# Matmul with RMS norm: transposes copied by two engines, two matmuls of a product placed earlier, and a reordered end

## The chip, the cores and the metric

The kernel runs on one core of a Trainium2 chip. The metric is the device time of one execution in microseconds (us), from the measured runs; the profile is of one further execution, taken by the hardware profiler. Engines are named as the profile names them: PE is TensorE (PEld its weight loads), DVE is VectorE, ACT is ScalarE, POOL is GpSimd and SP is SyncE. A bank is one of the eight parts of PSUM, the memory that PE writes; a tile of 128 x 512 fp32 fills one.

## The reference

```python
def setup_inputs():
    m, k, n = 2048, 2048, 2048
    return {
        "a": np.random.randn(m, k).astype(np.float32),
        "b": np.random.randn(k, n).astype(np.float32),
        "gamma": np.random.randn(n).astype(np.float32),
        "eps": np.float32(1e-5),
    }

def reference(a, b, gamma, eps):
    x = np.matmul(a, b)
    rms = np.sqrt(np.mean(x ** 2, axis=-1, keepdims=True) + eps)
    return (gamma * x / rms).astype(np.float32)
```

## The kernel before, in words

The 2048 rows of A are 16 row blocks of 128. The contraction is cut into 16 tiles of 128, taken in pairs: `kp` runs over 8 pairs. The 2048 columns are four chunks of 512, two to a half. PE needs A transposed, with the contraction on the partitions, so each 128x128 piece of A is turned by PE itself (a matmul with `is_transpose`) into PSUM and copied to SBUF, or is turned by a DMA later on. B arrives as bf16, in `raw[half][kp]`.

The order of the work is written out by hand (`manual_schedule`): each engine executes its instructions in the order of the program text. The program writes no semaphores; the tile layer derives the waits from the tiles that instructions read and write. `tbank` and `acc[0]` to `acc[6]` are the eight banks.

**Head, left half of the columns.** Row blocks 0 to 3 are multiplied while A and B are still loading. For each `kp`, `stream` issues 14 matmuls of 128x512 (seven pairs of row block and chunk, two tiles of the contraction) into `acc`. After the first `when` of them it calls `transpose_head(kp + 1)`: eight transposes (L182) into `tbank`, viewed as bf16 `(t, r, m)` with the two tiles `t` side by side in one bank, and one DVE copy (L187) of 128x1024 into `head_at`. The eighth pair of row block and chunk has no bank of its own: `stream_in_parts` computes it by two matmuls (L435) in `tbank`, the same bank as the transposes, and DVE adds it to an SBUF tile (L442; ACT copies it the first time, L439). After that DVE forms differences of quarters of B for later (`b_diff`, `b_rest`). The loads of A (`early`, L119) and B (L115) are issued by POOL, one behind the other. `transpose_first` (L167) does the first pair from fp32, with one bank for DVE and one for ACT. After the last `kp`, ACT and DVE evict the seven banks by turns (L445).

**Head, right half.** `stream_right(kp)` computes rows blocks 0 and 1 plainly (`first` and `second`, four matmuls each, into `acc[0]` to `acc[3]`) and, for row blocks 2 and 3, products of a Strassen-Winograd scheme: seven products of sums of quarters in place of eight. `product_matmul(g, j, m, bank, kp, start)` issues step `kp` of product `m` (L358); `product` runs all eight. Product 1 gathers in bank `u2`, product 2 in `u4`, product 7 in `p7`. Afterwards (L517 to L546) ACT copies `u2` to `x11`, product 6 is added into `u2`, DVE copies that to `u4`, products 3 and 5 follow. ACT evicts the first plain bank and then computes two row norms of the next row blocks (`row_norm`, L220); DVE turns these into scales (`row_factor`, L230) and scales A to fp16 (`row_apply`, L241), and PE transposes it (`transpose_half`, L195).

**Middle.** Pairs of row blocks go through the seven products, with sums, squares, norms and stores of earlier rows beside them (`segment`); some groups add a second level of the scheme (`step`, L397). The change does not touch this part.

**End.** `last_group` (L752) orders the last products, `do(n, m)`, by hand. `B2` and `B3` are banks; `b3[1]` holds the upper right result after product 5 of the right half, until ACT copies it to `x22[1]` (L810); product 3 of that half then accumulates into the same bank. `square_of` squares a chunk on ACT and sums it along the row. The last row block needs its whole sum of squares, then a root on ACT (L288) and a reciprocal on DVE (L293); the factor `r_b` scales four chunks: one on DVE (L855, with a store of its own), chunks 1 and 3 of the tile `wide` on ACT (`by_r`, L766, two instructions) and chunk 2 on DVE (L762). One store of 768 KB (L860) takes the last three.

Of the kernel before, what the change touches and what calls it, by code (L numbers as in the profile page):

```python
# [17 lines left out]
def kernel(  # L18
# [13 lines left out]
    nc = tc.nc  # L32
# [4 lines left out]
    KP = KT // 2  # L37
    W2 = 2 * P
    MB = M // P
    CH = 512  # L40
# [137 lines left out]
    def transpose_head(kp):  # L178
        view = tbank.bitcast(BF16).rearrange("p (t r m) -> p t r m", t=2, r=HB)
        for t in range(2):  # L180
            for r in range(HB):
                nc.tensor.matmul(  # L182
                    view[:, t, r, :], ah(kp)[:, r, t * P:(t + 1) * P], identity,
                    is_transpose=True,
                    start=(t == 0 and r == 0), stop=(t == 1 and r == HB - 1),
                )
        nc.vector.tensor_copy(out=head_at[:, 2 * kp:2 * kp + 2, :, :], in_=view)  # L187

    a16 = {}

# [74 lines left out]
    def x_chunk(mb, c):  # L265
        return x_tile(mb, c // 2)[:, (c % 2) * CH:(c % 2 + 1) * CH]
# [181 lines left out]
    for kp in range(KP):  # L448
        if kp + 4 < KP:
            load_head(kp + 4)  # L450
        else:
            load_later(1)
        before = [lambda: transpose_head(kp + 1)] if kp + 1 < KP else []
        if kp == KP - 2:
            before.append(lambda: a_sums(PAIR, (3,), False))
        stream(kp, before, len(groups1) + {0: 5, 1: 3}.get(kp, 2))
        if kp == KP - 1:
            evict(groups1, "ADADADA")
        stream_in_parts(last1, kp)
        if kp > 0:  # L460
            b_diff(0, kp - 1)
        if 0 < kp < KP - 2:
            b_rest(0, kp - 1)
# [8 lines left out]
    def stream_right(kp):  # L472
        first, second = ([(g, 2 * kp + t) for g in plain] for t in range(2))
        if kp == 0:
            for both in zip(first, second):
                for g, kt in both:
                    head_matmul(banks[g], *g, kt)
            product_matmul(PAIR, 1, 1, u2, kp, True)
            product_matmul(PAIR, 1, 2, u4, kp, True)
            return  # L480
        product_matmul(PAIR, 1, 1, u2, kp, True)
        for g, kt in first:
            head_matmul(banks[g], *g, kt)
        if kp == KP - 1:
            product_matmul(PAIR, 1, 7, p7, kp - 1, True)
        product_matmul(PAIR, 1, 2, u4, kp, True)
        if kp < KP - 1:
            product_matmul(PAIR, 1, 7, p7, kp - 1, True)
        for g, kt in second:
            head_matmul(banks[g], *g, kt)  # L490

    for kp in range(KP):
        load_later(1)
        b_diff(1, kp)
        stream_right(kp)
        if kp % 2 == 0:
            square_half(kp // 2, 0)
        if kp > 0:
            b_rest(1, kp - 1)
        if kp == 0:  # L500
            b_diff(0, KP - 1)
            b_rest(0, KP - 3)
        if kp == 1:
            b_rest(0, KP - 2)
            b_rest(0, KP - 1)
        if kp in (2, 3, 4):
            a_sums(PAIR, ((1,), (2,), (4,))[kp - 2])
# [4 lines left out]

    r2, r3 = HB - 2, HB - 1
    x11, x12, x21, x22 = (x_chunk(r, c) for r in (r2, r3) for c in (2, 3))
    copy_on("A")(out=x11, in_=u2)  # L517
    product_matmul(PAIR, 1, 7, p7, KP - 1, True)
    b_rest(1, KP - 1)
    add(x11, u4, x11)  # L520
    evict(plain[:1], "A")
    row_norm(HB)
    row_norm(HB + 1)
    product(PAIR, 1, 6, u2, start=False)
    nc.vector.tensor_copy(out=u4, in_=u2)
    row_factor(HB)
    row_apply(HB)
# [224 lines left out]
    def last_group():  # L752
        n = len(halves) - 2
        g = NG - 1
        ra, rb = 2 * g, 2 * g + 1
        x11, x12, x21, x22 = zip(chunks(n), chunks(n + 1))
        xa, xb = x_tile(ra, 0), x_tile(rb, 0)
        gam = [gamma_sb[:, c * CH:(c + 1) * CH] for c in range(NCH)]
        gam_left = gamma_sb[:, 0:HALF]

        def scaled_gamma(x, src, r, gamma_of_x):
            nc.vector.scalar_tensor_tensor(out=x, in0=src, scalar=r, in1=gamma_of_x,  # L762
                                           op0=ALU.mult, op1=ALU.mult)

        def by_r(x, r):
            nc.scalar.activation(out=x, in_=x, func=ACTF.Copy, scale=r)  # L766

        def by_r_pool(x, r):
            nc.gpsimd.tensor_scalar(out=x, in0=x, scalar1=r, scalar2=1.0,  # L769
                                    op0=ALU.mult, op1=ALU.mult)  # L770

        b2, b3 = [B2[(n + j) % 2] for j in range(2)], [B3[(n + j) % 2] for j in range(2)]
        x00, x01 = first_sums(n)[0:2]
        do(n, 6)
        step(g - 1, 1, X2)
        nc.scalar.copy(out=W2, in_=X2)
        square_right(rb - 2)
        do(n - 1, 3)
        step(g - 1, 2, W2)
        step(g - 1, 6, X2)  # L780
        nc.scalar.copy(out=Y2, in_=X2)
        finish(rb - 2)
        take(n - 1, 12)
        add(x00, W2, x00)
        do(n + 1, 1)
        step(g - 1, 5, Y2)
        step(g - 1, 7, W2)
        step(g - 1, 4, X2)
        square_half(ra - 2, 0)
        add(x11[1], Y2, x11[1])  # L790
        a_sums(g, (4,))
        add(x11[0], W2, x11[0])
        add(x11[1], W2, x11[1])
        take_pre(ra - 2)
        square_of(ra, x11[1])
        do(n, 5)
        nc.scalar.copy(out=x22[0], in_=b3[0])
        add(x11[0], X2, x11[0])
        step(g - 1, 3, Y2)
        add(x01, Y2, x01)  # L800
        square_right(ra - 2)
        do(n + 1, 6)
        finish(ra - 2)
        do(n, 7)
        add(x22[0], x21[0], x22[0])
        add(b2[0], b2[0], x21[0])
        square_of(rb, x22[0])
        add(x11[1], x11[1], gam[2], ALU.mult)
        do(n + 1, 5)
        nc.scalar.copy(out=x22[1], in_=b3[1])  # L810
        wide = a_pool.tile([P, K], FP32, name="a32")
        chunk = [wide[:, c * CH:(c + 1) * CH] for c in range(NCH)]
        add(chunk[1], x22[0], gam[1], ALU.mult)
        pre_b = stat_pool.tile([P, 1], FP32, name="part")
        add(pre_b, msq[rb][:, 0:1], msq[rb][:, 1:2])
        do(n, 3)
        take(n, 12)
        square_half(ra, 0)
        pre_a = stat_pool.tile([P, 1], FP32, name="pre")
        nc.vector.tensor_scalar(out=pre_a, in0=msq[ra][:, 0:1], scalar1=msq[ra][:, 1:2],  # L820
                                scalar2=msq[ra][:, 2:3], op0=ALU.add, op1=ALU.add)
        add(xa, xa, gam_left, ALU.mult)
        do(n + 1, 3)
        take(n + 1, 12)
        square_of(ra, x12[1])
        rms_a = root(msq[ra][:, 3:4], pre_a)
        r_a = inverse(rms_a)
        other = X2
        product(g, 1, 7, other)
        nc.scalar.copy(out=x21[1], in_=other)  # L830
        left, mid = xa[:, 0:CH], xa[:, CH:]
        by_r(left, r_a)
        nc.sync.dma_start(out=rows(ra, 0, CH), in_=left)
        by_r_pool(mid, r_a)
        nc.sync.dma_start(out=rows(ra, CH, HALF), in_=mid)
        by_r_pool(x11[1], r_a)
        add(b2[1], b2[1], x21[1])
        add(x22[1], x21[1], x22[1])
        scaled_gamma(x12[1], x12[1], r_a, gam[3])
        nc.sync.dma_start(out=rows(ra, HALF, N), in_=x_tile(ra, 1))  # L840
        do(n, 4)
        square_of(rb, b2[0])
        square_of(rb, x22[1])
        add(xb[:, 0:CH], b2[0], gam[0], ALU.mult)
        part = stat_pool.tile([P, 1], FP32, name="part")
        nc.vector.tensor_scalar(out=part, in0=pre_b, scalar1=msq[rb][:, 2:3],
                                scalar2=msq[rb][:, 3:4], op0=ALU.add, op1=ALU.add)
        add(chunk[3], x22[1], gam[3], ALU.mult)
        do(n + 1, 4)
        last_sq = stat_pool.tile([P, 1], FP32, name="last_sq")  # L850
        sq = sq_pool.tile([P, 2 * CH], BF16, name="sq")
        nc.scalar.activation(out=sq[:, 0:CH], in_=b2[1], func=ACTF.Square, scale=inv_sqrt_n,
                             accum_out=last_sq)
        r_b = inverse(root(last_sq, part))
        nc.vector.tensor_scalar_mul(out=xb[:, 0:CH], in0=xb[:, 0:CH], scalar1=r_b)  # L855
        nc.sync.dma_start(out=rows(rb, 0, CH), in_=xb[:, 0:CH])
        for c in (1, 3):
            by_r(chunk[c], r_b)
        scaled_gamma(chunk[2], b2[1], r_b, gam[2])
        nc.sync.dma_start(out=rows(rb, CH, N), in_=wide[:, CH:])  # L860

# [38 lines left out]
```

## Time and profile before

| | |
|---|---|
| median of 3 runs (lowest to highest) | 219.31 us (219.22 to 220.76) |
| profiled execution | 219.36 us |
| its span, first to last instruction | 217.6 us |
| PE busy | 207.6 us, 95% of the span |
| DVE busy | 161.6 us, 74% |
| ACT busy | 113.3 us, 52% |
| POOL busy | 35.3 us, 16% |
| granted PE clock, mean | 0.99 |

In the lines of the profile, `L187 DVE COPY head_at<-tbank 128x1024 bf16<-128x1024 bf16 x7` is line 187 of the kernel, the engine, the operation, the tile written and the tile read, their shapes, and how often. Lines of a timeline begin with the start and the duration in us and end, in brackets, with the idle time of the engine just before and what ended it; neighbouring instructions of one kind are merged into one line. Durations of matmuls overlap, since PE is pipelined: 512 columns show about 0.38 us each and start 0.216 us apart. PEld is the weight load ahead of a matmul. The chain that ended last is followed back from the last instruction, at each step to what released it.

### The profile page before, as it was taken

The numbers are of one execution on the slowest core, as the hardware profiler recorded it, in microseconds if no ns is written. First come the engines' busy times: TensorE is split into PE (matmuls) and PEld (weight loads), VectorE is DVE, ScalarE is ACT, GpSimd is POOL, SyncE is SP. The second block draws the span as 40 slices with busy tenths as digits, with TensorE's granted clock in tenths as the row PEclk, the third lists the DMA queues.
The fourth block names the chain that finished last, engine by engine and source line by source line (L and its number), as shares of the span: only waits on it lengthen the run. The fifth ranks groups of instructions, "written<-read, shape, count | busy, mean of one in ns | idle before, by whom it ended". The sixth has DMA issues, their size and how long they took to land.

```text
span 217.6 us, 2966 instructions
## 1 busy us (share of the span) xinstructions
PE 207.6 (95%) x1016; PEld 95.9 (44%) x1016; DVE 161.6 (74%) x323; ACT 113.3 (52%) x223; POOL 35.3 (16%) x74
## 2 busy tenths in 40 slices
PE   7899999999999999999999999999999999999970
PEld 3344544444455444444444444444444444444420
DVE  1227769999899997788975899399856985475771
ACT  2110001910599579498626962594728951555772
POOL 7644434434001000100021001100101000000020
PEclk9999999999999999999999999999999999999996
DMA  7999999999969798978674975497596992040454
GB/s 151 167 200 204 203 205 209 209 211 211 399 220 358 295 264 230 334 294 240 163 234 167 350 246 99 184 245 240 118 268 237 326 261 50 0 193 3 193 191 195
DMA packets 37039, 46.60 MB, mean 214 GB/s; under 512 B 22560, under 2 KB 26656, under 8 KB 35744
## 3 DMA queue, kind: packets, MB, share of 16 engines
q0 software_dynamic: 10608, 23.86, 45.5%
q1 hardware_dynamic: 26144, 22.29, 33.7%
q10 hardware_dynamic: 272, 0.26, 0.3%
q8 instruction: 8, 0.13, 0.2%
q14 instruction: 7, 0.06, 0.1%
HBM read 34.60 MB, written 16.78 MB: 236 GB/s over the span
## 4 chain that ended last, share of the span: by engine, by line
PE 85%; DMA 9%; POOL 2%; issue 1%; ACT 1%; ACTq 0%; DVE 0%; POOLq 0%
PE acc L358 65%; PE acc L406 11%; DMA early<-in_a_dram 5%; DMA b<-in_b_dram 4%; PE acc L397 3%; PE tbank L397 2%; POOL b L115 1%; PE tbank L358 1%; PE tbank L435 1%; PE tbank L182 1%; POOL early L119 1%; PE tbank L195 0%; PE acc L195 0%; ACT a L766 0%; ACTq L895 0%
## 5 line engine op out<-in xcount | busy, mean ns | idle before, releaser
L358 PEld LDWEIGHTS <-s 128*128 128x128 f16 (+1 forms) x312 | 30.5, 98 | 37.0 <-DVE s L335 0.3
L272 ACT ACTIVATE sq<-x 128x1024 bf16<-128x1024 f32 (+1 forms) x33 | 33.2, 1005 | 24.8 <-DVE x L101 20.9
L406 PE MATMUL acc<-b,head_at 128*128 128x512 bf16 x176 | 43.0, 379 | 0.9 <-DMA b<-in_b_dram 0.7
L311 DVE SCALAR_TENSOR_TENSOR x<-x,r,gamma_sb 128x1024 f32<-128x1024 f32 x28 | 34.9, 1282 | 0.5
L358 PE MATMUL acc<-b,head_at 128*128 128x512 bf16 x136 | 33.9, 379 | 0.0
L101 DVE TENSOR_TENSOR x<-acc,x 128x512 f32<-128x512 f32 x33 | 22.3, 687 | 11.4 <-PE acc L358 5.4
L358 PEld LDWEIGHTS <-head_at 128*128 128x128 f16 (+1 forms) x192 | 18.7, 98 | 22.2
L358 PE MATMUL acc<-b,at_even 128*128 128x512 bf16 x112 | 26.3, 379 | 0.0
L406 PEld LDWEIGHTS <-head_at 128*128 128x128 bf16 x176 | 16.9, 98 | 20.1 <-issue 1.0
L358 PE MATMUL acc<-early,s 128*128 128x512 bf16 x104 | 25.5, 379 | 0.0
L358 PE MATMUL acc<-b,s 128*128 128x512 bf16 x104 | 24.6, 379 | 0.0
L358 PEld LDWEIGHTS <-at_even 128*128 128x128 f16 x160 | 15.6, 98 | 18.6
L224 ACT ACTIVATE sq<-a 128x1024 bf16<-128x1024 f32 x22 | 23.3, 1058 | 0.6 <-DMA a<-in_a_dram 0.2
L358 PE MATMUL acc<-t_left,s 128*128 128x512 bf16 x96 | 22.7, 379 | 0.0
L115 POOL DMA_DIRECT2D b<-in_b_dram x32 | 17.2, 541 | 20.4 <-DMA b<-in_b_dram 14.3
L445 ACT COPY x<-acc 128x512 f32<-128x512 f32 x7 | 4.0, 581 | 25.8 <-PE acc L406 25.8
L587 ACT COPY acc<-acc 128x512 f32<-128x512 f32 x12 | 6.9, 576 | 10.4 <-PE acc L358 10.4
L187 DVE COPY head_at<-tbank 128x1024 bf16<-128x1024 bf16 x7 | 4.8, 691 | 8.1 <-PE tbank L182 8.1
L293 DVE RECIPROCAL r<-rms 128x1 f32<-128x1 f32 x16 | 2.6, 160 | 10.6 <-ACT rms L288 10.6
L101 DVE TENSOR_TENSOR x<-tbank,x 128x512 f32<-128x512 f32 x9 | 6.2, 690 | 4.2 <-PE tbank L435 4.1
L589 ACT COPY x<-acc 128x512 f32<-128x512 f32 x10 | 5.9, 585 | 5.3 <-PE acc L358 5.3
L769 POOL TENSOR_SCALAR x<-x,r 128x512 f32<-128x512 f32 x2 | 1.4, 691 | 41.9 <-DVE r L293 41.9
(129 smaller groups left out, 240.5 us busy)
## 6 DMA issues: line engine op xcount, KB each, us to landing
out_dram<-x SPq DMA_DIRECT2D x29, 512.0 KB, 3.0
a<-in_a_dram POOLq DMA_DIRECT2D x9, 1024.0 KB, 5.5
b<-in_b_dram POOLq DMA_DIRECT2D x32, 256.0 KB, 9.9
a<-in_a_dram POOLq DMA_DIRECT2D x4, 512.0 KB, 10.0
early<-in_a_dram POOLq DMA_DIRECT2D x7, 256.0 KB, 10.2
gamma_sb<-in_gamma_dram POOLq DMA_DIRECT2D x2, 512.0 KB, 10.1
head_at<-in_a_dram POOLq DMA_DIRECT2D x1, 1024.0 KB, 8.2
out_dram<-x SPq DMA_DIRECT2D x3, 256.0 KB, 2.6
```

What stands on the lines that cost most here:

```text
L101: nc.vector.tensor_tensor(out=out, in0=in0, in1=in1, op=op)
L115: nc.gpsimd.dma_start(out=raw[j][kp][:, t, :], in_=b[lo:lo + P, j * HALF:(j + 1) * HALF])
L187: nc.vector.tensor_copy(out=head_at[:, 2 * kp:2 * kp + 2, :, :], in_=view)
L224: nc.scalar.activation(out=junk, in_=a32[mb][:, h * HALF:(h + 1) * HALF], func=ACTF.Square, scale=2.0 ** -8, accum_out=n2[:, h:h + 1])
L272: nc.scalar.activation(out=sq[:, 0:src.shape[-1]], in_=src, func=ACTF.Square, scale=inv_sqrt_n, accum_out=msq[mb][:, c:c + 1])
L311: nc.vector.scalar_tensor_tensor(out=x, in0=x, scalar=inverse_of[mb], in1=gamma_sb[:, h * HALF:(h + 1) * HALF], op0=ALU.mult, op1=ALU.mult)
L358: nc.tensor.matmul(bank, lhsT[:, kp, :], rhs, start=(start and kp == 0), stop=(kp == KP - 1), skip_group_check=not start)
L397: nc.tensor.matmul(bank, lhsT[:, k, :], rhs, start=(m in (1, 7) and k == 0), stop=(k == KQ - 1), skip_group_check=m not in (1, 7))
L406: nc.tensor.matmul(bank, head_at[:, kt, r, :], head_rhs(c, kt), start=(kt == 0), stop=(kt == KT - 1))
L445: copy_on(engine)(out=x_chunk(*g), in_=banks[g])
L587: nc.scalar.copy(out=b3, in_=b2)
L589: nc.scalar.copy(out=chunks(n)[2], in_=B7)
```

## The change

It has five edits in three places.

In `transpose_head` the one DVE copy of both tiles becomes a DVE copy of tile 0 and an ACT copy of tile 1. In the loop over `kp`, the transposes stand behind 10 of the 14 matmuls for every `kp` from 1 (before: 10 for `kp` 1 and 9 from `kp` 2), and behind 12 for `kp` 0 as before.

In `stream_right`, at the last `kp`, the ACT copy of `u2` stands behind `first` in program order, and the first two matmuls of product 6 follow product 7, ahead of product 2 and `second`. The loop after it issues the other six.

In `last_group` the copy of `b3[1]` to `x22[1]` goes ahead of the square of `x22[0]` on ACT, and the two scalings of chunks 1 and 3 become one instruction over both.

```diff
@@ transpose_head @@
-        nc.vector.tensor_copy(out=head_at[:, 2 * kp:2 * kp + 2, :, :], in_=view)
+        nc.vector.tensor_copy(out=head_at[:, 2 * kp, :, :], in_=view[:, 0])
+        nc.scalar.copy(out=head_at[:, 2 * kp + 1, :, :], in_=view[:, 1])
@@ loop over kp @@
-        stream(kp, before, len(groups1) + {0: 5, 1: 3}.get(kp, 2))
+        stream(kp, before, len(groups1) + (5 if kp == 0 else 3))
@@ stream_right @@
         if kp == KP - 1:
+            copy_on("A")(out=x11, in_=u2)
             product_matmul(PAIR, 1, 7, p7, kp - 1, True)
+            for k in range(2):
+                product_matmul(PAIR, 1, 6, u2, k, False)
         product_matmul(PAIR, 1, 2, u4, kp, True)
@@ after the loop over stream_right @@
-    copy_on("A")(out=x11, in_=u2)
     product_matmul(PAIR, 1, 7, p7, KP - 1, True)
...
-    product(PAIR, 1, 6, u2, start=False)
+    for kp in range(2, KP):
+        product_matmul(PAIR, 1, 6, u2, kp, False)
@@ last_group @@
-        square_of(rb, x22[0])
         add(x11[1], x11[1], gam[2], ALU.mult)
         do(n + 1, 5)
         nc.scalar.copy(out=x22[1], in_=b3[1])
+        square_of(rb, x22[0])
...
-        for c in (1, 3):
-            by_r(chunk[c], r_b)
+        by_r(wide.rearrange("p (c n) -> p c n", n=CH)[:, 1::2, :], r_b)
```

The lines that name `x11`, `x12`, `x21` and `x22` move above the loop and are otherwise the same.

More of the change, by code (lines that the diff above doesn't have):

```diff
@@ L490, in stream_right @@
             head_matmul(banks[g], *g, kt)
+    r2, r3 = HB - 2, HB - 1
+    x11, x12, x21, x22 = (x_chunk(r, c) for r in (r2, r3) for c in (2, 3))
     for kp in range(KP):
@@ L511 @@
     load_block(HB + 2)
-    r2, r3 = HB - 2, HB - 1
-    x11, x12, x21, x22 = (x_chunk(r, c) for r in (r2, r3) for c in (2, 3))
-    copy_on("A")(out=x11, in_=u2)
     product_matmul(PAIR, 1, 7, p7, KP - 1, True)
```

## The prediction

> **What bounds the kernel now.** I read the busy shares first, then the chain that ended last, then the timeline of the three places that the diff touches.
>
> ```profile
> PE 207.6 (95%) x1016; PEld 95.9 (44%) x1016; DVE 161.6 (74%) x323; ACT 113.3 (52%) x223; POOL 35.3 (16%) x74
> ...
> PE 85%; DMA 9%; POOL 2%; issue 1%; ACT 1%; ACTq 0%; DVE 0%; POOLq 0%
> ```
>
> The chain is TensorE (PE) for 85%. In order of time it leaves PE only before 26.02 us, where it waits for the loads of A, and after 210.57, where the last row factor is computed. Between these two points PE issues a 512-column matmul every 0.216 us with one gap (0.14 us, below). So every tenth of a microsecond that PE loses after 26 us reaches the end, and what it gains before 26 us may run into the loads.
>
> The head, one step of `stream` (kp = 4 in the middle; its first and last steps around it):
>
> ```profile
> 9.86 0.62 PE L182 MATMUL tbank<-identity,early 128*128 128x128 bf16 x8
> ...
> 11.26 0.59 PE L435 MATMUL tbank<-b,head_at 128*128 128x512 bf16 x2 [0.35 <-DVE head_at L187]
> ...
> 26.02 0.62 PE L182 MATMUL tbank<-identity,early 128*128 128x128 bf16 x8 [0.19 <-DMA early<-in_a_dram]
> 26.48 1.24 PE L406 MATMUL acc<-b,head_at 128*128 128x512 bf16 x5
> 26.68 0.69 DVE L187 COPY head_at<-tbank 128x1024 bf16<-128x1024 bf16 x1 [0.35 <-PE tbank L182]
> 27.56 0.59 PE L435 MATMUL tbank<-b,head_at 128*128 128x512 bf16 x2
> 27.99 2.11 PE L406 MATMUL acc<-b,head_at 128*128 128x512 bf16 x9
> 29.93 0.61 PE L182 MATMUL tbank<-identity,early 128*128 128x128 bf16 x8
> ...
> 35.36 0.59 PE L435 MATMUL tbank<-b,head_at 128*128 128x512 bf16 x2
> ```
>
> Call T the start of the eight transposes (L182). They issue in 0.45 us and end at T+0.62; VectorE (DVE) copies tbank from T+0.66 to T+1.35; PE meanwhile has five matmuls (1.08 us), so L435, which writes tbank again, is due at T+1.54, and the copy (free for PE at about T+1.40) is just hidden. At 9.86 only two matmuls lay between, and PE did wait, 0.35 us.
>
> **Part 1: the split copy.** 128x1024 on DVE becomes 128x512 on DVE and 128x512 on ScalarE (ACT). DVE: 0.42 us (the L176 casts, 256 fp32 columns, and the bf16 adds of 128x512 both show 415 to 426 ns; half of 0.69 would be 0.35, the lower bound). ACT: 0.585 us (L439, L445 and L517 show 0.581 to 0.587 for 512 columns; L202, 1024 columns, 1.012 less the 0.43 by which a 1024 square exceeds a 512 one, gives 0.585).
>
> The question is whether they lie side by side. Both read tbank, which is one bank. No wait is written in the kernel, the tile layer derives them, and the trace shows how: by the bank, not by the bytes.
>
> ```profile
> 5.38 0.38 PE L172 MATMUL acc<-t_left,early 128*128 128x128 f32 x2
> ...
> 5.38 0.60 PE L172 MATMUL acc<-t_left,early 128*128 128x128 f32 x4
> ...
> 6.02 0.65 ACT L176 CAST head_at<-acc 128x256 bf16<-128x256 f32 x2 [3.28 <-PE acc L172]
> ```
>
> The first of the two ACT casts reads only the first two transposes, done at 5.76. It starts at 6.02, after the fourth (5.98). The same function gives DVE and ACT a bank each. I find no place in the trace where the two read one bank at the same time, so two readers at once are not shown, and the nearest row says that users of a bank take turns. I take series: DVE first, as in the program's order, then ACT.
>
> The Trainium skill ("PSUM — Partial Sum Buffer", section on bank collisions) speaks against this change: two engines that read one bank and the same partitions at once collide, read against read included, and give wrong data, so a scheduler has to order them. By that rule the copies come one after the other, by the change's own layout they run together; the times for both are worked out below from the rows.
>
> In series L435 can start at T + 0.66 + 0.42 + 0.04 + 0.585 + 0.05 = T+1.755 (handovers: DVE 202.21 to ACT 202.24 and DVE 211.86 to ACT 211.95, so 0.03 to 0.09; ACT 203.44 to PE 203.49). The moved call leaves only four matmuls as cover, due at T+1.31, so PE stands 0.45 us in each step; two matmuls and ten more follow until the next T, 12 x 0.216 = 2.59. A step is 4.35 us; it was 3.90, or the loads' pace. From the first T, 9.86 (not changed), with 0.06 more at kp = 1, where DVE started at T+0.72: the last L435 of this kind starts at 9.86 + 7 x 1.755 + 0.06 + 6 x 2.59 = 37.75 instead of 35.36: **+2.39 us**. The T between are 14.21, 18.61, 22.96, 27.30, 31.65, 35.99, all later than the loads that released the transposes (13.69, 17.85, 21.70, 26.02, 29.89, 33.70), so the loads hide nothing. DVE saves 7 x 0.27 us, which no one waits for: in series its add and four subtractions after L435 end at T+4.88, 0.13 before the next copy could start. ACT has nothing else until 36.85. The later place of the transposes (at 10 matmuls instead of 9 for kp from 2) would gain its 0.216 us only where PE waits for loads. Bounds: DVE 0.35 to 0.42 and handovers up to 0.06 longer give 1.685 to 1.815 a step, so +1.9 to +2.8.
>
> **Part 2: two matmuls of product 6 sooner.** PE's work is the same and it had no gap there, so nothing is gained on PE itself. The ACT copy of u2 runs where it ran (56.06 to 56.65) and the first sooner matmul comes five matmuls after product 1, 1.08 us, so it does not wait: cost nothing. But the four `second` matmuls come 0.43 later, and with them the first eviction, which leads ACT's queue:
>
> ```profile
> 57.58 0.59 ACT L445 COPY x<-acc 128x512 f32<-128x512 f32 x1 [0.92 <-PE acc L406]
> ...
> 63.38 0.14 DVE L232 TENSOR_SCALAR s<-norm 128x1 f32<-128x1 f32 x1
> ...
> 65.41 0.64 PEld L195 LDWEIGHTS <-a_first 128*128 128x128 f16 x8
> 65.61 0.61 PE L195 MATMUL tbank<-identity_h,a_first 128*128 128x128 f16 x8
> ```
>
> Behind it ACT runs both row_norms without a gap up to 63.27; DVE takes the second norm at 63.38, scales until 65.36, and PE's transposes load at 65.41 for 65.61. ACT 0.43 later gives the norm at 63.70, DVE 0.35 later, weights at 65.76: PE waits about 0.16, and then about 0.04 before product 7 (loaded at 68.60 right behind DVE's sum, for 68.66). **+0.20 us**; between 0 (if ACT had slack I don't see) and 0.43.
>
> **Part 3: the end.**
>
> ```profile
> 202.24 0.63 ACT L272 ACTIVATE sq<-x 128x512 bf16<-128x512 f32 x1 [1.57 <-DVE x L101]
> ...
> 202.87 0.57 ACT L810 COPY x<-acc 128x512 f32<-128x512 f32 x1
> ...
> 203.49 3.12 PEld L358 LDWEIGHTS <-s 128*128 128x128 f16 x15 [0.27 <-issue]
> ...
> 211.95 1.33 ACT L766 ACTIVATE a<-a,r 128x512 f32<-128x512 f32 x2 [0.28 <-DVE r L293]
> ...
> 213.31 0.33 SPq L860 DMA_DIRECT2D out_dram<-a  x1
> ```
>
> Product 3 of the right half writes the bank that L810 reads. It was due at 201.61 + 8 x 0.216 = 203.34; its weights load at 203.49, behind the copy (203.44). This is the gap: 16 matmuls to 205.21 took 3.60, not 3.45. Ahead of the square the copy needs only PE's 201.77, ends at 202.40, and the square still ends before ACT's next copy at 203.54. **-0.14 us**, bounds -0.14 to 0; ACT's copy of product 7 comes 0.11 sooner, so DVE's add before the last product still ends 0.12 ahead of it. The one scaling of 1024: 0.72 plus the same 0.43 is 1.155 against 1.33: **-0.17**; the limits are DVE's part beside it (212.30 + 0.74, so -0.24) and no gain. Both are on the chain up to the last store.
>
> **Sum**, on the profiled run's 219.36 (span 217.6 and 1.8 around it; the median is 219.31): 219.36 + 2.39 + 0.20 - 0.31 = **221.6**. With the bounds: 219.36 + 1.9 + 0 - 0.38 = 220.9 to 219.36 + 2.8 + 0.43 = 222.6.
>
> **The rivals.** (a) The two copies run side by side. ACT would end at T + 0.66 + 0.585 = T+1.25, PE be free at T+1.30, against T+1.31 due: no wait, just. Then the head gains one matmul at the load wait of 26.02 (0.2 us) and loses it again in part 2, where PE comes 0.2 sooner to weights that come 0.2 later; the end gives -0.31: 219.05. It decides if ACT starts by T+0.67. For it: the transposes placed one matmul later fit exactly this. Against: the bank rows above. 14%. (b) Series, and DVE late too: its 0.13 us of slack is gone if each of its ops takes 0.06 more, and the steps stretch by some 0.2: about 222.8. 3%. (c) Series, but the small terms kind (handovers at 0.03, no wait in the middle): 219.36 + 2.3 - 0.31 = 221.35, inside the forecast's range.
>
> **Chances.** 1% is 2.19 us, about what a measurement of this kernel can tell from no change; slower begins at 221.50. Series holds 83%; its sum lies 0.14 above that bound with some 0.3 of doubt, so I put 56% above and 27% below. With (a) wholly within 1%, and (b) above: slower 0.59, same 0.40, faster 0.01. The range 220.9 to 222.6 leaves out (a), (b) in part and the tails.
>
> **What would show it.** Right: ACT's copy starts at DVE's end and not beside it; L435 waits for ACT in all seven steps, T's spacing is 4.35, and the transposes' waits for loads are gone; PE is 2.4 late by 40 us, 2.6 by 70. The gap before product 3 of the right half is gone, and one 128x1024 scaling of about 1.15 stands before the last store. Wrong: ACT's copy starts with DVE's, and PE reaches 40 us where it was or sooner.

## The result, and the profile after

The changed kernel takes 222.94 us (median of 6 runs, 221.99 to 225.18), the kernel before 219.5 us (6 runs, 219.12 to 220.76): 1.0164 times the time before, with a 95% interval of 1.0132 to 1.0197. It is slower, as forecast, but by 3.4 us where 2.3 were forecast, and its median lies 0.34 above the range. Two further comparisons gave 222.0 (1.0132) and 222.3 us (1.0141), inside the range; what differs between the three is a good part of this study.

The execution that was profiled is the slowest of the six: 225.18 us, with a span of 223.4. I read it in the order in which the prediction argued. First the busy times, and from the chain that ended last its shares by engine:

```profile
PE 208.4 (93%) x996; PEld 96.3 (43%) x1016; DVE 160.0 (72%) x323; ACT 117.2 (52%) x229; POOL 35.2 (16%) x74
...
PE 86%; DMA 6%; ACT 3%; DVE 1%; issue 1%; ACTq 0%; DVEq 0%; POOLq 0%
```

PE's work is the same (208.4 us busy against 207.6; this trace lacks the records of 20 of the 1016 matmuls), but its share of the span falls from 95% to 93%. ACT, 1% of the chain before, is 3% now: PE waits for it. Where, the waits say, of PE for the whole span and of ACT from 10 to 41 us (total, times, longest):

```profile
PE tbank L436 <- ACT head_at L188: 2.4, 7, 0.7
PE acc L359 <- DMA head_at<-a: 1.0, 1, 1.0
...
ACT head_at L188 <- DVE head_at L187: 28.1, 7, 6.8
```

In all seven steps of the head ACT's half of the copy waits for DVE's half, and PE waits for ACT's. The timeline of the head shows it in one step, with the first and the last around it (L182 the transposes, L187 and L188 the two copies, L436 the two matmuls into `tbank`):

```profile
7.94 4.44 PE L407 MATMUL acc<-b,head_at 128*128 128x512 bf16 x12 [2.14 <-DMA b<-in_b_dram]
12.22 0.61 PE L182 MATMUL tbank<-identity,early 128*128 128x128 bf16 x8
...
13.96 0.59 PE L436 MATMUL tbank<-b,head_at 128*128 128x512 bf16 x2 [0.70 <-ACT head_at L188]
...
29.61 0.61 PE L182 MATMUL tbank<-identity,early 128*128 128x128 bf16 x8
30.06 1.03 PE L407 MATMUL acc<-b,head_at 128*128 128x512 bf16 x4
30.26 0.42 DVE L187 COPY head_at<-tbank 128x512 bf16<-128x512 bf16 x1
30.72 0.59 ACT L188 COPY head_at<-tbank 128x512 bf16<-128x512 bf16 x1 [3.74 <-DVE head_at L187]
31.35 0.59 PE L436 MATMUL tbank<-b,head_at 128*128 128x512 bf16 x2 [0.27 <-ACT head_at L188]
...
33.94 0.61 PE L182 MATMUL tbank<-identity,early 128*128 128x128 bf16 x8
...
40.01 0.59 PE L436 MATMUL tbank<-b,head_at 128*128 128x512 bf16 x2 [0.27 <-ACT head_at L188]
```

DVE copies from 30.26 to 30.68, ACT from 30.72 to 31.31, and L436 starts at 31.35, T+1.74. The next transposes come at 33.94, one step of 4.33 us later. No transposes wait for a load any more. What is new is the beginning: PE waited 2.14 us for its first load of B, then took 4.28 us for 12 matmuls that need 2.6 at 0.216 each, and the first T is 12.22 where the kernel before had 9.86. The last L436 starts at 40.01, before at 35.36.

The middle and the end, from the same timeline:

```profile
68.38 0.15 DVE L233 TENSOR_SCALAR s<-norm 128x1 f32<-128x1 f32 x1
...
70.42 0.45 PEld L196 LDWEIGHTS <-a_first 128*128 128x128 f16 x8 [0.49 <-DVE a_first L244]
...
183.41 1.04 PE L359 MATMUL acc<-b,head_at 128*128 128x512 bf16 x4 [0.99 <-DMA head_at<-a]
...
207.60 3.62 PE L359 MATMUL acc<-b,s 128*128 128x512 bf16 x16
207.80 0.59 ACT L813 COPY x<-acc 128x512 f32<-128x512 f32 x1 [1.14 <-PE acc L359]
208.28 0.63 ACT L273 ACTIVATE sq<-x 128x512 bf16<-128x512 f32 x1
...
217.78 1.15 ACT L770 ACTIVATE a<-a,r 128x1024 f32<-128x1024 f32 x1 [0.28 <-DVE r L294]
```

The weights of the middle's transposes now wait for DVE's scaling. At 183.41 PE stands 1.0 us for a piece of A that a DMA transposes; the kernel before has no such gap. The 16 matmuls from 207.60 run without one, the copy stands ahead of the square, and one scaling of 1.15 us replaces two.

The last two stores are issued as follows, the first of them in the kernel before (whose last one, at 213.31, stands in the prediction), then both in the changed kernel:

```profile
212.41 0.33 SPq L856 DMA_DIRECT2D out_dram<-x  x1
```

```profile
218.25 0.33 SPq L860 DMA_DIRECT2D out_dram<-x  x1
218.96 0.33 SPq L863 DMA_DIRECT2D out_dram<-a  x1
```

Counted from the start of the 16 matmuls, the last store is issued 0.34 us sooner (218.96 − 207.60 = 11.36, against 213.31 − 201.61 = 11.70). But the span ends 4.46 us after that issue, where it was 4.27 (to the hundredth it is 223.42 and 217.58 us long), so only half of the 0.34 reaches the time. In all twelve traces of this study the span ends 5.13 to 5.17 us after the issue of the store before the last, whether the last one follows 0.70 us behind it (with the one scaling) or 0.90 (with two). So the 0.19 us by which the one scaling frees the last store sooner is worth nothing in the time; why, no run shows.

The difference between the two profiled executions is 5.82 us. It comes together as follows: first transposes later, 12.22 − 9.86 = 2.36; from there to the last L436, 27.79 against 25.50, 2.29; the middle 0.17 (product 7 at 73.48 against 68.66 is 4.82 later, of which 4.65 were there at L436); the late wait and smaller ones beside it 1.17 in all; the end −0.17. The sum is 5.82. So two terms of this execution, 2.36 and 1.17, stood in no step of the forecast. The text of the program before the first transposes is the same in both kernels.

### The profile page after: what moved, and what is told of

The parts are those of the page before. It is cut to its first block, busy times and chain, and to the rows that moved or that the text cites. A ratio compares the mean times of both kernels' runs of the same rounds, so it can differ in the third digit from the quotient of the medians.

```text
span 223.4 us, 2957 instructions
## 1 busy us (share of the span) xinstructions
PE 208.4 (93%) x996; PEld 96.3 (43%) x1016; DVE 160.0 (72%) x323; ACT 117.2 (52%) x229; POOL 35.2 (16%) x74
## 4 chain that ended last, share of the span: by engine, by line
PE 86%; DMA 6%; ACT 3%; DVE 1%; issue 1%; ACTq 0%; DVEq 0%; POOLq 0%
PE acc L359 61%; PE acc L407 15%; PE acc L398 3%; DMA b<-in_b_dram 3%; DMA head_at<-a 3%; PE tbank L398 2%; PE tbank L436 2%; ACT head_at L188 2%; PE tbank L182 2%; DVE head_at L187 1%; PE tbank L359 1%; ACT a L770 1%; PE tbank L196 0%; PE acc L196 0%; ACT sq L856 0%
## 5 line engine op out<-in xcount | busy, mean ns | idle before, releaser
L188 ACT COPY head_at<-tbank 128x512 bf16<-128x512 bf16 x7 | 4.1, 586 | 28.1 <-DVE head_at L187 28.1
L187 DVE COPY head_at<-tbank 128x512 bf16<-128x512 bf16 x7 | 3.0, 425 | 11.4 <-PE tbank L182 10.7
L593 ACT COPY x<-acc 128x512 f32<-128x512 f32 x10 | 5.9, 585 | 5.3 <-PE acc L359 5.3
```

The source lines that it names most:

```text
L187: nc.vector.tensor_copy(out=head_at[:, 2 * kp, :, :], in_=view[:, 0])
L188: nc.scalar.copy(out=head_at[:, 2 * kp + 1, :, :], in_=view[:, 1])
L593: nc.scalar.copy(out=chunks(n)[2], in_=B7)
```

## The experiments

**The changed kernel once more.** Two theories: A, the late beginning and the late DMA wait belong to the execution; B, the change causes them. No edit.

> The changed kernel once more, for a second trace. In the first one the last L436 of the split kind came 4.65 us late: 2.36 were there at the first transposes already (12.22 instead of 9.86 us), and the seven steps gave 2.29. Another 1.0 us was lost at 183 us, where PE waited for a DMA transpose. Theory A (chance): both belong to that one execution; here the first transposes start near 9.9, the wait at 183 is gone, the steps again give 2.3, and the profiled run takes 219.36 + 2.29 + 0.17 - 0.34 = 221.5. Theory B (cause): both follow from the change; then they are here again and the run takes about 225.

222.0 us (4 runs, 221.89 to 223.05) against 219.38 (20 runs): 1.0132 (1.0097 to 1.0167). The lines of the profiled execution (221.97 us), from PE's timeline:

```profile
9.98 0.62 PE L182 MATMUL tbank<-identity,early 128*128 128x128 bf16 x8
...
37.78 0.59 PE L436 MATMUL tbank<-b,head_at 128*128 128x512 bf16 x2 [0.27 <-ACT head_at L188]
```

The head begins at 9.98 and the last L436 is at 37.78, again 27.8 later; no wait near 183 us stands in PE's waits. With a T0 (so I call the first transposes' start) 0.12 later than before, the terms give 219.36 + 0.12 + 2.30 + 0.17 + 0.20 − 0.17 = 221.98, measured 221.97. The 0.20 are a small late wait: at 186.26 PE waits for a sum of DVE that waited for a DMA transpose of A. Theory A holds for the beginning. Of the late wait it shows that the changed kernel can be nearly without it.

**One copy again, the transposes as in the change.** This separates the split from the new place of the transposes (behind 10 matmuls for every `kp`).

```diff
-        nc.vector.tensor_copy(out=head_at[:, 2 * kp, :, :], in_=view[:, 0])
-        nc.scalar.copy(out=head_at[:, 2 * kp + 1, :, :], in_=view[:, 1])
+        nc.vector.tensor_copy(out=head_at[:, 2 * kp:2 * kp + 2, :, :], in_=view)
```

> The change with one DVE copy of 128x1024 again, all else as changed. Theory of the bank (copies in series cost the head 2.3 us): the copy ends at T+1.40 and four matmuls end at T+1.31, so a step that doesn't wait for loads loses 0.09, the load wait at 26.02 is back and gains most of a matmul: head +0.04, middle +0.17, end -0.34: 219.36 - 0.13 = 219.2, ratio 0.999. Rival: the later place of the transposes is what costs (too little cover for any copy): then this stays above 221.

219.56 us (10 runs) against 219.38: 1.0001 (0.998 to 1.0022). Without the split the cost is gone, as far as the interval of some 0.45 us to either side can tell. In the trace L435 comes at T+1.39 to T+1.40 from the third transposes on, and the steps are 3.98 us; that one execution began very late (T0 14.11, total 224.66) and is used for durations alone.

**The split alone, in the kernel before.**

```diff
-        nc.vector.tensor_copy(out=head_at[:, 2 * kp:2 * kp + 2, :, :], in_=view)
+        nc.vector.tensor_copy(out=head_at[:, 2 * kp, :, :], in_=view[:, 0])
+        nc.scalar.copy(out=head_at[:, 2 * kp + 1, :, :], in_=view[:, 1])
```

> The kernel before with the split copy alone, transposes after 9 matmuls from kp = 2 as before. Copies in series: L435 can't start before T+1.755, whatever lies between; one matmul more stands in the cover and one less before the next T, so from kp = 1 a step is 1.755 + 11 x 0.216 = 4.13 (the first 4.35): the last L435 of the kind at 36.7 against 35.36, +1.3 us, nothing at middle and end: 220.7, ratio 1.006. Rival (parallel copies): no change or 0.2 less.

221.43 us (5 runs, 220.8 to 222.12), 1.0095 (1.0065 to 1.0125), 0.7 above what I expected. In the trace the expected step stands: 4.11 us, last L436 at T0 + 26.73 (expected 26.8):

```profile
30.97 0.61 PE L182 MATMUL tbank<-identity,early 128*128 128x128 bf16 x8
...
35.08 0.61 PE L182 MATMUL tbank<-identity,early 128*128 128x128 bf16 x8
...
36.83 0.59 PE L436 MATMUL tbank<-b,head_at 128*128 128x512 bf16 x2
```

The rows show PE waiting for ACT in two of the steps only, since they count from the end of the last matmul, and the fifth matmul ends just before the copies do; L436 still comes at T+1.74 or T+1.75 in the others (36.83 − 35.08), where the pace of issue alone would give T+1.53. The traced execution has T0 10.10 and took 220.8; the other runs are up to 1.3 above it, which no trace explains. So each step is as expected, and the sum from T0 = 9.86 is too low here too.

**The two sooner matmuls alone, in the kernel before.**

```diff
         if kp == KP - 1:
+            copy_on("A")(out=x11, in_=u2)
             product_matmul(PAIR, 1, 7, p7, kp - 1, True)
+            for k in range(2):
+                product_matmul(PAIR, 1, 6, u2, k, False)
...
-    product(PAIR, 1, 6, u2, start=False)
+    for kp in range(2, KP):
+        product_matmul(PAIR, 1, 6, u2, kp, False)
```

> The kernel before with the two matmuls of product 6 placed sooner and nothing else. Theory: ACT's eviction and both row norms come 0.43 later, PE waits for the scaled rows at 65.6: about +0.17 us, 219.5, ratio 1.001, PE's only new gap there. Rival: the sooner matmuls cover a late load of B in the head and nothing is lost: 219.3 or less, no gap at 65.6.

219.39 us (10 runs), 1.0006 (0.999 to 1.0022): the 0.2 us is below what the times resolve. The trace has it:

```profile
65.95 0.45 PEld L195 LDWEIGHTS <-a_first 128*128 128x128 f16 x8 [0.49 <-DVE a_first L243]
65.96 0.62 PE L195 MATMUL tbank<-identity_h,a_first 128*128 128x128 f16 x8
```

The weights wait for DVE and the transposes start 0.35 later than before (65.61), in an execution in which the last L435 was 0.18 later: 0.17 from the edit. This trace also has a wait of 0.82 us at 184.83 (DVE, for a DMA transpose of A, and PE behind it), with none of the other edits in it. The first transposes and the last L435 of this execution, for the comparison further down:

```profile
10.59 0.62 PE L182 MATMUL tbank<-identity,early 128*128 128x128 bf16 x8
...
35.54 0.59 PE L435 MATMUL tbank<-b,head_at 128*128 128x512 bf16 x2
```

**Both kernels with a later beginning.** Sixteen warm-up matmuls in place of eight, in the kernel before and in the changed one. If the kernel before can absorb a late start in its waits for loads and the changed one can't, the difference between the two grows.

```diff
-    for _ in range(8):
+    for _ in range(16):
         nc.tensor.matmul(acc[0], warm[:, 0:P], warm[:, 0:CH], start=True, stop=True)
```

> The kernel before with 16 warm-up matmuls in place of 8, so that PE alone starts later and the loads stay where they are. Theory (pass-through): with T0 the start of the first transposes, PE reaches the fifth ones at T0 + 15.63 if nothing holds it, and their load lets them start at 26.02, so the first 0.5 us of lateness past 9.86 are lost in the waits for loads; the last L435 of the kind shifts by T0 - 10.39, not by T0 - 9.86. The time rises by about 0.5 less than T0. Rival: the lateness reaches the end in full here too.

> The changed kernel with the same 16 warm-up matmuls. Theory (pass-through): its steps wait for copies and never for loads, so the last L436 of the kind comes at T0 + 27.8 whatever T0 is, and the time rises by the whole lateness of T0. Against the late kernel before, the split then costs 2.9 in the head and not 2.4, and the two late kernels differ by about 2.8 us, 1.3%, where 2.3 was forecast. Rival (nothing passes): they differ by 2.3.

The kernel before: 219.88 us (10 runs) against 219.54 without the warm-ups (29 runs), 1.0018 (0.9991 to 1.0045). The changed kernel: 222.69 (4 runs), 2.81 above it. PE's timeline of the first, and of the second:

```profile
10.44 0.62 PE L182 MATMUL tbank<-identity,early 128*128 128x128 bf16 x8
...
35.50 0.59 PE L435 MATMUL tbank<-b,head_at 128*128 128x512 bf16 x2
```

```profile
10.60 0.61 PE L182 MATMUL tbank<-identity,early 128*128 128x128 bf16 x8
...
38.39 0.59 PE L436 MATMUL tbank<-b,head_at 128*128 128x512 bf16 x2 [0.27 <-ACT head_at L188]
```

In the kernel before a start 0.58 later (10.44 for 9.86) moves the last L435 by 0.14 (35.50 for 35.36). In the changed one the last L436 is at T0 + 27.79, to the hundredth what it was at T0 12.22. So the same late start costs the changed kernel all of itself. With it the head's difference is 38.39 − 35.50 = 2.89, or 2.73 if the second had begun at 10.44 as well.

**The split with more cover.** The transposes stand three matmuls sooner, so that seven lie between them and L436: a way to keep the split without PE's wait.

```diff
-        stream(kp, before, len(groups1) + (5 if kp == 0 else 3))
+        stream(kp, before, len(groups1) + (5 if kp == 0 else 0))
```

> The changed kernel with the transposes after 7 of the 14 matmuls from kp = 1, so that seven lie between them and L436: due at T+1.96, later than the serial copies free the bank (T+1.755). Theory (copies in series, the cost is their length over the cover): no wait at L436 from kp = 1; the load waits are back, each in front of 7 matmuls of cover instead of 5, so the last L436 of the kind comes 0.4 late; with the middle's 0.17 and the end's -0.34 that is 219.6, ratio 1.001. Rival (ACT's copy or the extra wait costs PE by itself): 221 or more.

220.51 us (10 runs, 219.96 to 221.46), 1.0038 (1.001 to 1.0065): most of the cost is gone, but not all, against an expectation of none. The timeline of the last step:

```profile
34.25 0.61 PE L182 MATMUL tbank<-identity,early 128*128 128x128 bf16 x8
...
34.98 0.42 DVE L101 TENSOR_TENSOR t_left<-b,t_left 128x512 bf16<-128x512 bf16 x1
...
35.33 0.41 DVE L187 COPY head_at<-tbank 128x512 bf16<-128x512 bf16 x1
35.78 0.59 ACT L188 COPY head_at<-tbank 128x512 bf16<-128x512 bf16 x1 [3.52 <-DVE head_at L187]
...
36.41 0.59 PE L436 MATMUL tbank<-b,head_at 128*128 128x512 bf16 x2
```

The transposes were done at 34.86, but DVE still had a subtraction to do and began its copy at T+1.08; the chain of the two copies then ends at T+2.12, beyond seven matmuls, and L436 comes at T+2.16 where T+1.96 was due. Four of the seven steps are like this (T+2.14 to T+2.17). This is the prediction's rival (b), DVE late, at another place: moving the transposes sooner moves the copy into DVE's subtractions. The last L436 is at 36.41, 1.05 later than in the kernel before at an equal T0 (9.85); I had expected 0.4.

**The end's edits alone, in the kernel before.**

```diff
-        square_of(rb, x22[0])
         add(x11[1], x11[1], gam[2], ALU.mult)
         do(n + 1, 5)
         nc.scalar.copy(out=x22[1], in_=b3[1])
+        square_of(rb, x22[0])
...
-        for c in (1, 3):
-            by_r(chunk[c], r_b)
+        by_r(wide.rearrange("p (c n) -> p c n", n=CH)[:, 1::2, :], r_b)
```

> The kernel before with the edits of the end alone: the copy ahead of the square, and one scaling of 128x1024. The gap of 0.14 before product 3 of the right half closes and the scaling takes 1.15 in place of 1.33, so the last store leaves 0.3 sooner: 219.0, ratio 0.9985, faster than both kernels. Rival: other waits behind them take the gain, 219.3.

219.31 us (12 runs) against 219.54, 0.9998 (0.9973 to 1.0023): a gain of 0.3 us isn't resolved. The timeline of the end has both edits at their forecast size:

```profile
201.26 3.62 PE L358 MATMUL acc<-b,s 128*128 128x512 bf16 x16
...
211.45 1.15 ACT L766 ACTIVATE a<-a,r 128x1024 f32<-128x1024 f32 x1 [0.28 <-DVE r L293]
```

The 16 matmuls show 3.62 us in place of 3.76, with no gap of 0.14, and the scaling 1.15 in place of 1.33. Of the 0.34 us by which the last store is issued sooner, the time again has half: the head of this execution is 0.35 shorter (last L435 at 35.01 for 35.36), and 219.36 − 0.35 − 0.17 = 218.84, which is what it took, the fewest of its twelve. If any version here beats the kernel before, it is this one, but that isn't shown.

**A bank for each half.** Does the bank set the order of the two copies, or something else, such as the order of the program? The second tile's transposes go into a bank of their own. There is none free, so one of the seven pairs of row block and chunk is left out: the pair's products are not computed and its place in the result is filled from another pair. The time is not comparable (an eighth of the matmuls of the left half's head is missing); the question is only when ACT starts.

```diff
-        view = tbank.bitcast(BF16).rearrange("p (t r m) -> p t r m", t=2, r=HB)
+        view = [bank.bitcast(BF16)[:, 0:CH].rearrange("p (r m) -> p r m", r=HB)
+                for bank in (tbank, acc[6])]
...
+        nc.vector.tensor_copy(out=head_at[:, 2 * kp, :, :], in_=view[0])
+        nc.scalar.copy(out=head_at[:, 2 * kp + 1, :, :], in_=view[1])
...
-    groups1 = [(r, c) for r in range(HB) for c in range(2)][:-1]
+    groups1 = [(r, c) for r in range(HB) for c in range(2)][:-2]
```

> The changed kernel with one of the seven pairs of row block and chunk left out of the head (row block 3, chunk 0: its result is a copy of another pair's), so that a bank is free and the transposes of tile 1 go to it: two banks, one for each engine; four matmuls lie between transposes and L436 as in the change. Theory (the order is by bank): ACT's copy now starts beside DVE's, at about T+0.66, and the wait of L436 for ACT (0.27 in each step from kp = 2) is gone. Rival (ACT waits for DVE for another reason, its output tile for one): it still starts at T+1.1. The time can't be compared, since the work is less.

A step from the timeline:

```profile
30.34 0.40 PE L183 MATMUL tbank<-identity,early 128*128 128x128 bf16 x4 [0.23 <-DMA early<-in_a_dram]
...
30.77 0.42 DVE L188 COPY head_at<-tbank 128x512 bf16<-128x512 bf16 x1
...
31.00 0.59 ACT L189 COPY head_at<-acc 128x512 bf16<-128x512 bf16 x1 [3.29 <-PE acc L183]
...
31.66 0.59 PE L437 MATMUL tbank<-b,head_at 128*128 128x512 bf16 x2
```

ACT doesn't wait for DVE but for PE's last transpose of its own bank, and starts 0.23 us after DVE, beside it. L437 follows at T+1.32 with no wait, against T+1.74 in the changed kernel. The same two instructions, of the same shapes and in the same order of the program, are in series with one bank and side by side with two. It is the bank (each bank is one tile here, so whether the tile layer goes by the tile or by the bank can't be told apart).

**The changed kernel a third time**, with more executions, since two comparisons had given 1.0164 and 1.0132.

> The changed kernel a third time, with more executions, to place its median. With the sum corrected for the start (the last L436 at T0 + 27.8, the last L435 of the kernel before at 35.0 to 35.5 for T0 up to 10.6) the change costs 2.4 us in an execution that starts at 9.86 and 2.9 in one that starts at 10.4 or later, with the middle's 0.17 and the end's -0.34 net 2.25 to 2.75: a median of 221.7 to 222.3 against 219.4 to 219.5, ratio 1.010 to 1.0125. Rival (something more is lost that the traces of quiet executions don't show): a ratio of 1.016 as in the first comparison.

222.3 us (6 runs, 221.95 to 223.04) against 219.24 (12 runs): 1.0141 (1.0116 to 1.0165), above the 1.010 to 1.0125 that I expected. Its profiled execution has T0 10.26, the last L436 at 38.06 (T0 + 27.80) and 0.13 us of late wait: 219.36 + 0.40 + 2.30 + 0.17 + 0.13 − 0.17 = 222.19, measured 222.20.

## Why the prediction was right and wrong

**The copies in series: right.** The forecast put L435 at T+1.755, with PE waiting 0.45 us in each step and a step of 4.35; the traces show T+1.74 and 4.33. The rows show 0.27 of the 0.43 that PE loses (30.06 + 4 x 0.216 = 30.92, and L436 at 31.35), since they count from the end of the last matmul, which is 0.17 later than the pace of issue. From the first T to the last L436 it forecast 27.89 us, and every trace of the changed kernel has 27.79 or 27.80. The reason holds too: the nearest row (a cast of two transposes that waited for all four of its bank) spoke for an order by the bank, and the experiment with two banks shows it. The rule of the Trainium skill that the prediction set beside it ("PSUM — Partial Sum Buffer", bank collisions: a scheduler has to put two readers of one bank in order) agrees with the 7 of 7 waits; that the two would collide if left unordered, no run here shows. Rival (a), side by side, falls.

**The middle: right; the end: half of it.** For the middle +0.20 was forecast, and it is 0.17 in the changed kernel and in the edit alone. For the end −0.31 was forecast. Up to the issue of the last store it is −0.34, but the time has −0.17: the closed gap (forecast −0.14) counts, the one scaling (forecast −0.17, with "no gain" as a limit) does not. The forecast followed both to the last store and stopped there, and the span does not end sooner when that store is issued sooner behind the one before it.

**The head's +2.39, counted "From the first T, 9.86 (not changed)" against 35.36: wrong, and this is the step that failed.** The mechanism was right and the size of the term was off, on both sides of its subtraction. The text up to T0 isn't changed, but T0 is no constant of it. In the nine traces with the same text up to there it was 9.85, 9.86, 9.93, 9.98, 10.10, 10.26, 10.59, 12.22 and 14.11, as the first loads landed, those of B above all (and in the last two with a lower clock behind that wait, see the end); the forecast took the second earliest and put a later start at nothing. And the 25.50 us from T0 to the last L435 in that execution contain waits for loads: the third transposes (17.86) came 0.17 later than PE's own step of 3.84 from 13.85, the fifth (26.02) 0.35 later than 3.90 from 21.77, 0.52 in all:

```profile
13.85 0.61 PE L182 MATMUL tbank<-identity,early 128*128 128x128 bf16 x8
...
17.86 0.62 PE L182 MATMUL tbank<-identity,early 128*128 128x128 bf16 x8
...
21.77 0.61 PE L182 MATMUL tbank<-identity,early 128*128 128x128 bf16 x8
```

In the other traces with one copy at its old place these waits are smaller, and the head shorter. The table has T0, the last matmul pair in `tbank` of this kind, and the distance:

| trace | T0 | last L435 or L436 | from T0 |
|---|---|---|---|
| before | 9.86 | 35.36 | 25.50 |
| before, the end's edits | 9.93 | 35.01 | 25.08 |
| before, 16 warm-ups | 10.44 | 35.50 | 25.06 |
| before, two matmuls sooner | 10.59 | 35.54 | 24.95 |
| changed, second comparison | 9.98 | 37.78 | 27.80 |
| changed, third comparison | 10.26 | 38.06 | 27.80 |
| changed, 16 warm-ups | 10.60 | 38.39 | 27.79 |
| changed, first comparison | 12.22 | 40.01 | 27.79 |

The kernel before can hide up to half a microsecond of a late start in its waits for loads. The changed kernel has no such waits and passes on all of it. So the change costs 2.84 us of PE's time in the head (27.79 − 24.95), and what is seen is that less the waits for loads that the kernel before still had: 2.3 in the execution that I predicted from, 2.7 to 2.8 in the others. Of the 2.84, the split alone has 1.78 (26.73 − 24.95, the experiment with the split alone); the other 1.06 come with the later place of the transposes, which takes one matmul from the cover in each step from `kp` 2 on. With one copy the same later place costs only 0.40 (from the second transposes to the last L435 21.36 in the experiment without the split, 20.96 in the one with the two matmuls sooner). The forecast saw the fact ("the loads hide nothing") and took it for a simplification of its sum; it did not draw the consequence for the other kernel, nor set a term for a later T0.

The four traced executions of the changed kernel (the last with 16 warm-ups), in the forecast's terms:

| term, us | forecast | first comparison | second | third | 16 warm-ups |
|---|---|---|---|---|---|
| T0 later than 9.86 | 0 | 2.36 | 0.12 | 0.40 | 0.74 |
| from T0 to the last L436, against 25.50 | 2.39 | 2.29 | 2.30 | 2.30 | 2.29 |
| middle | 0.20 | 0.17 | 0.17 | 0.17 | 0.17 |
| late waits for DMA transposes | 0 | 1.17 | 0.20 | 0.13 | 0.07 |
| end | −0.31 | −0.17 | −0.17 | −0.17 | −0.17 |
| sum on 219.36 | 221.6 | 225.18 | 221.98 | 222.19 | 222.46 |
| measured | | 225.18 | 221.97 | 222.20 | 222.47 |

The three terms that the forecast did size come to 2.28 there and to 2.29 or 2.30 here. That they agree to 0.02 is luck: the end's gain was forecast 0.14 too large, and the other two costs together 0.12 to 0.13 too large. What the forecast missed are the two terms that it put at nothing.

**The rest of the first comparison's 222.94.** Its profiled execution, 225.18 us, has 2.36 us of late start and 1.17 of late DMA waits in it. The other five are 221.99 to 223.62 and have no trace; that they hold smaller amounts of the same is argued, not shown. In the two later comparisons these amounts were 0.3 to 0.5 us in the traced executions, and their medians lie inside the range; why the first comparison had more of them, no trace shows.

**What stays open** is whether the change has a share in the late waits for DMA transposes. In the four traced executions of the whole change they cost 1.17, 0.20, 0.13 and 0.07. In its parts and variants PE waits 0.82 (the sooner matmuls alone), 0.70 (without the split) and not at all in four; in the two of the kernel before it doesn't wait. In the execution that lost 1.17 us the two DMA transposes ahead of that wait took 1.99 and 3.04 us to issue, in the kernel before 1.43 and 1.53. The changed kernel arrives there 2.5 to 5 us later than the one before, beside other transfers, but the 0.82 came in a kernel that was 0.35 late. Sorted by edit, all six traces with such a wait are of kernels with the two sooner matmuls; two more traces with them have none, and the four traces without them have none either. That points at this edit, but no mechanism is shown, and its own ten executions have a median equal to the kernel before. Twelve traces don't settle it.

## What to carry to other kernels

Before a read of one PSUM bank is split between two engines, count the two halves one behind the other (here 0.42 + 0.04 + 0.59 us, against 0.69 for the whole on VectorE), or give each half its own bank. When an edit takes away the waits for loads early in a kernel, it also takes away the slack that hides a late start, so the cost is PE's whole loss and not the difference from one trace: count the waits that the kernel before had there, and leave room upward in the range for a later start. Follow a gain at the end past the issue of the last store to the end of the span: here 0.34 us up to the issue were 0.17 in the time.

## What the runs showed of the hardware that was not expected

**The PE clock falls after a wait of 2.14 us.** In the profiled execution of the changed kernel PE waited 2.14 us for its first load of B, after 3.5 us of warm-up matmuls and 1 us of transposes. The table by stretches of 2 us (stretch, its length, busy time and number of instructions of PE, PEld, DVE, ACT and POOL, granted clock, DMA share, GB/s):

```profile
8.00:10.00 2.00, 2.00 (x6) 0.73 (x6) 0.00 (x0) 0.00 (x0) 0.89 (x2) 0.52 1.27 195
10.00:12.00 2.00, 2.00 (x7) 0.71 (x6) 0.00 (x0) 0.00 (x0) 1.14 (x6) 0.62 1.16 204
```

The clock granted is 0.52 and 0.62 of full speed, and the 512-column matmuls start 0.43 us apart, not 0.216. In finer stretches it falls to 0.50 at 8.1 us, just after PE has begun again, and is back at 1.00 at 11.5, 3.4 us later. Two other executions show the same: with two banks, after a wait that came to 2.80 us, it was 0.50 from 7.6 to 11.0, 3.4 us; with one copy, after 3.30 us, from 8.0 to 14.8, 6.8 us, twice as long. In all three the fall came 2.1 to 2.3 us after the wait began. After waits of 1.71 us and less the clock stayed at 1.00. Of the 2.36 us by which the first execution began late, some 1.7 are the slow clock (4.28 us for 12 matmuls, less 2.6 at 0.216 each) and the rest the load.

The Trainium skill ("TensorE: Matmul & The Clock Gate", Part 1, what is actually happening) says that the clock is halved after an idle window of about 3.4 us, and that the window runs freely. The 3.4 and 6.8 us at the low clock agree with a window of that length. But PE had been idle for only 2.1 to 2.2 us when the clock fell, so here a wait of 2.14 us was enough, and the measurement decides.

**A DVE copy of half the columns takes more than half the time**: 0.42 us for 512 bf16 columns from PSUM, 0.69 for 1024. With ACT's 0.59 for the other half, the split would have been worth some 0.1 us a step at best even side by side, an estimate from 0.69 against 0.59.
